# Reordering the early steps, the softmax steps and the first two output blocks of a hybrid attention block

## The chip, the cores and the metric

The kernel runs on one core of one Trainium2 chip. The metric is the device time of one execution in microseconds (us), the median over several runs. PE is TensorE, which multiplies matrices; DVE is VectorE, ACT is ScalarE, POOL is GpSimd, and SP issues transfers.

## What is computed

The reference is one decoder block over 512 positions of width 2048, in float32:

```
hn    = rmsnorm(x, norm1_g);  proj = hn @ w_in
o_a   = dilated_mixture(q_a, k_a, v_a)                # 8 heads, three dilated windows mixed by their sums
kc,vc = compress_blocks(k_c), compress_blocks(v_c)    # silu(flat @ w1) @ w2 over blocks of 32, stride 16
o_b   = sum of gates * (compressed, selected, window) # 8 heads, 2 groups of keys and values
h     = x + concat(rmsnorm(o_a), rmsnorm(o_b)) @ w_out
h     = h + (silu(hn2 @ w_gate) * (hn2 @ w_up)) @ w_down,  hn2 = rmsnorm(h)
out   = rmsnorm(h, final_g)
```

`compress_blocks` adds a position code to each of 32 positions of a block before the product with `w1`. All attention scores carry a distance penalty (`bias`).

## The kernel before

Everything is kept transposed: 128 features on the partitions, 512 positions on the free dimension. Each float32 operand is split into a high part (`h`, made by ACT as a rounded copy) and a low part (`l`, made by DVE as the difference), and a product is three matmuls: high times high, low times high, high times low (`mm3`, L165 to L167). `ah` and `al` hold the 16 blocks of the input of the current product, `wh` and `wl` the split weights.

The weights arrive in units of 512 KB (`raw`, four buffers, `load_to`). A unit is split in two halves of 128x512, each a `Job`: `first` is ACT's copy into `wh` (L136), `second` DVE's difference into `wl` (L139). `next_half` takes the next half for PE; before that it lets ACT split the half three further on and DVE the half two further on (`split_to`). `wh` and `wl` have five buffers each. `later(n, f)` puts `f` off to the start of the n-th half after the current one. The order of the units is written out by hand in `plan()`, and the scheduling is manual: each engine executes its instructions in the order in which the program emits them.

The stages touched:

1. After the input's norm factor `r1` is known (58.7 us into the profiled execution), the compression inputs are made from four PSUM banks `pc` in eight parts (`kv_part`): DVE multiplies a bank by `r1` (L333, `tmp`), adds position codes into `ku` (L341), ACT rounds it into `kvs` (L343), DVE takes the low part (L328). The parts are run from `side_hook`, one after every second column block of a projection. `gates_out` multiplies the gate projection `pg` by `r1` (L360) and transposes it on PE (L363, `pgt`). Meanwhile PE computes the projections ks, kw, vs and vw (`pp`), each in two units of 24 matmuls, and between them 16 units of the compression weights `w1` (`phid`, L382 and L383); `W1_AFTER` says how many follow each unit. `compressed` turns the result (`phidt`, two Silu, `pcmp`) when ten and twelve units are done. After each projection `evac` multiplies by `r1` and splits (L431, L437, L438).
2. Eight times, PE computes four projections and, between every six matmuls of them (`step`), one step of the attention heads in hand: scores of a tile (`s`, or `cmp_s` in the compressed branch), transposes of the exponentials (`t`), products with the values (`pv`, tile `po`). In a score step DVE adds the bias and takes the row minimum (L502, L551), ACT takes the exponential and its sum (L504, L554), and DVE inverts the sum and scales (L477 to L482, L556 to L559). A tile that was scored is transposed three steps later at the earliest (`SLACK`).
3. When the last head's value projection is half done, `split_act` turns the outputs `osb` of mixer B into the inputs `ah`, `al` 0 to 7 of the output projection (L254, L255), two per half. The output projection (`pab`) runs over 16 blocks for these inputs, two halves of four inputs each, while the last heads still take their steps, and later over 16 blocks for the other eight inputs. `close_attention` computes the group norms when all heads are done.
4. The feed-forward part follows, from 700 us to the end; nothing of it is changed.

Of the kernel before, what the change touches and what calls it, by code (L numbers as in the profile page):

```python
# [11 lines left out]
F32 = mybir.dt.float32  # L12
F32R = mybir.dt.float32r
AF = mybir.ActivationFunctionType
OP = mybir.AluOpType
# [3 lines left out]
KB = D // 128  # L19
# [16 lines left out]
NCMP = 31  # L36
MH, ML, WH, WL = 32, 32, 16, 16


W1_AFTER = {"ks": (0, 0), "kw": (3, 3), "vs": (3, 3), "vw": (2, 2)}  # L40


def plan():
# [28 lines left out]
def block_kernel(ctx: ExitStack, tc: tile.TileContext, xt, wst, wdn, smalls, wg, w2c, bias, ident_in, out):  # L72
# [76 lines left out]
                jobs.append(Job(half_of(u, k), load=lambda u=u: load_to(u + 1), even=True))  # L149

    n_plain = len(jobs)
    total = n_plain + 14 * FB + KB * NPH

    def split_to(n):
# [28 lines left out]
    def later(n, f):  # L183
        i = len(lag)
        while i and lag[i - 1][0] > pos["half"] + n:
            i -= 1
        lag.insert(i, (pos["half"] + n, f))
# [5 lines left out]
    def run_unit(subs):  # L193

        for k in range(0, len(subs), 4):
            h, l = next_half()
            for s in range(4):
                o, mh, ml, st, sp_ = subs[k + s]
                mm3(o, h[:, 128 * s:128 * s + 128], l[:, 128 * s:128 * s + 128], mh, ml, st, sp_)
                if s % 2:  # L200
                    side_hook[0]()
# [73 lines left out]
    def tmp(name="tmp"):  # L275
        return ap_.tile([128, S], F32, tag="tmp", name=name, bufs=3)
# [53 lines left out]
    def kv_part(s, g, v):  # L330
        if not v:
            kv_src[0] = tmp()
            dve.tensor_tensor(kv_src[0], pc[2 * s + g], r1, op=OP.mult)  # L333
        tv = kv_src[0].rearrange("p (c i) -> p i c", i=16)
        c = (SM_PK, SM_PV)[s] + 16 * v
        u = cp.tile([128, S], F32, tag="ku", name="ku", bufs=2)
        uv = u.rearrange("p (i c) -> p i c", i=16)
        n = 32 - v
        if v:
            pool_e.memset(uv[:, :, 31:], 0.0)  # L340
        dve.tensor_tensor(uv[:, :, :n], tv[:, :, v:], sm[:, c:c + 16, None].to_broadcast([128, 16, n]), op=OP.add)  # L341
        h, l = (kvs[:, s, v, :, i, g, :] for i in range(2))
        act.activation(h, uv, AF.Copy)  # L343
        kv_low()
        pend.append((l, uv, h))
# [9 lines left out]

    side_hook[0] = task

    def gates_out():
        t = tmp()
        dve.tensor_tensor(t[:48, :], pg[:48, :], r1[:48, :], op=OP.mult)  # L360
        p = ps.tile([128, 4, 128], F32, tag="misc", name="pgt")
        for b in range(4):
            pe.transpose(p[:, b, :48], t[:48, 128 * b:128 * b + 128], ident[:48, :48])  # L363
        act.activation(gates, p[:, :, :24], AF.Copy)
        dve.tensor_tensor(gates, gates, p[:, :, 24:48], op=OP.add)
        act.activation(gates, gates, AF.Sigmoid)
# [96 lines left out]
    class Att:  # L463
# [20 lines left out]
        def s(self, tiles):  # L484
            p = ps.tile([128, 512], F32, tag="sc", name="psc", bufs=2)
            e = late["pool"].tile([128, 128 * sum(t + 1 for t in tiles)], F32, tag=f"e{tiles[0]}", name="e")
            st = late["pool"].tile([128, 4], F32, tag="st", name="st", bufs=4)
            o = 0
            qh, ql = self.q[:2]
            kh, kl = self.k  # L490
            for t in tiles:
                n = 128 * max(t + 1, 2)
                mm3(p[:, o:o + n], qh[:, 128 * t:128 * t + 128], ql[:, 128 * t:128 * t + 128],
                    kh[:, :n], kl[:, :n], True, True)
                o += n
            o = 0
            oe = 0
            for c, t in enumerate(tiles):
                n = 128 * (t + 1)
                et = e[:, oe:oe + n]  # L500
                m, den = st[:, 2 * c:2 * c + 1], st[:, 2 * c + 1:2 * c + 2]
                dve.tensor_tensor_reduce(et, p[:, o:o + n], self.bias[:, 384 - 128 * t:512], 1.0, 3e38,  # L502
                                         OP.add, OP.min, m)
                act.activation(et, et, AF.Exp, bias=m, scale=-1.0, accum_out=den)  # L504
                self.scale_rows(et, den, t, self.kind == "win")
                self.e[t] = et
                o += 128 * max(t + 1, 2)
                oe += n

        def t(self, tiles):  # L510
            p = ps.tile([128, 512], F32, tag="t", name="pt", bufs=2)
# [30 lines left out]
        def cmp_s(self):  # L542
            p = ps.tile([128, 512], F32, tag="sc", name="psc", bufs=2)
            e = late["pool"].tile([128, 4, 32], F32, tag="ec", name="ec")
            e3 = late["e3"]
            st = late["pool"].tile([128, 16], F32, tag="stc", name="stc", bufs=2)
            q = self.q[2]
            for t in range(4):
                pe.matmul(p[:, 32 * t:32 * t + 32], q[:, 128 * t:128 * t + 128], self.k, start=True, stop=True)
            for t in range(4):  # L550
                dve.tensor_tensor_reduce(e[:, t, :NCMP], p[:, 32 * t:32 * t + NCMP],  # L551
                                         self.bias[:, 512 + 32 * t:512 + 32 * t + NCMP], 1.0, 1e29, OP.add,
                                         OP.min, st[:, t:t + 1])
                act.activation(e[:, t, :NCMP], e[:, t, :NCMP], AF.Exp, bias=st[:, t:t + 1], scale=-1.0,  # L554
                               accum_out=st[:, 4 + t:5 + t])
            dve.tensor_scalar(st[:, 4:8], st[:, 4:8], 1e-30, None, op0=OP.max)  # L556
            dve.reciprocal(st[:, 4:8], st[:, 4:8])
            for t in range(4):
                dve.tensor_scalar(e3[:, t, :, :NCMP], e[:, t, None, :NCMP].to_broadcast([128, 3, NCMP]),  # L559
                                  st[:, 4 + t:5 + t], gates[:, t, self.gate:self.gate + 1],  # L560
                                  op0=OP.mult, op1=OP.mult)

        def cmp_t(self):
            p = ps.tile([128, 512], F32, tag="t", name="pt", bufs=2)
# [10 lines left out]

    queue = deque()
    now = [0]
    cur = {"s": None, "t": None, "ready": deque(), "turn": 0}
    SLACK = 2

    def step():

        now[0] += 1
        for _ in range(2):
            turn = cur["turn"]
            cur["turn"] ^= 1
            if turn == 0:
                if cur["t"] is None and cur["ready"] and cur["ready"][0][0] + SLACK < now[0]:
                    cur["t"] = cur["ready"].popleft()[1]
                    cur["ti"] = 0  # L590
                    cur["tat"] = -9
                a = cur["t"]
                if a is not None:
                    is_pv = cur["ti"] == len(a.t_steps) - 1
                    if is_pv and (cur["tat"] + SLACK > now[0] or (a.v is not None and not a.v.ready())):
                        continue
                    a.t_steps[cur["ti"]]()
                    cur["tat"] = now[0]
                    cur["ti"] += 1
                    if cur["ti"] == len(a.t_steps):  # L600
                        cur["t"] = None
                    return True
            else:
                if cur["s"] is None and queue and len(cur["ready"]) == 0:
                    if isinstance(queue[0], Att):
                        cur["s"] = queue.popleft()
                        cur["si"] = 0
                    else:
                        queue.popleft()()
                        return True  # L610
                a = cur["s"]
                if a is not None:
                    t = cur["t"]
                    if t is not None and t.kind != "cmp" and a.kind != "cmp" and cur["ti"] <= cur["si"]:
                        continue
                    a.s_steps[cur["si"]]()
                    cur["si"] += 1
                    if cur["si"] == len(a.s_steps):
                        cur["s"] = None
                        cur["ready"].append((now[0], a))  # L620
                    return True
        return False
# [71 lines left out]
    for j in range(NH):  # L694
# [25 lines left out]
        for half in range(2):  # L720
            in_unit(p, half)
            if j == NH - 1 and half == 0:
                for i in range(8):
                    later(i // 2, lambda i=i: split_act(i, osb[:, 8 + i, :], sm[:, SM_GB + i:SM_GB + i + 1]))
        t = evac_v(p)
# [160 lines left out]
    side_hook[0] = last_steps  # L886
    term = {}
    pab = []
    for nb in range(KB):
        while "hs" not in rest and (nb == 4 and not idle() or nb == 2 and (queue or cur["s"])):  # L890
            step()
        p = out_unit(1, ("proj", "sc", "t")[nb // 2 % 3])
        if "hs" in rest:
            later(0, lambda nb=nb, p=p: add_b(nb, p))
        else:
            pab.append((nb, p))
# [355 lines left out]
```

## Time and profile before

| | |
|---|---|
| Median of 3 runs | 2183.11 us (2182.37 to 2186.63) |
| Profiled execution, its own time | 2182.41 us |
| Its span in the trace | 2180.6 us |
| Granted TensorE clock, mean | 0.998 |
| PE, DVE, ACT, POOL busy | 2161.7, 1568.4, 970.5, 43.7 us |
| Read from and written to HBM | 225.51 MB, 4.19 MB |

Times inside the execution count from the start of the span. A row of the order of time gives the start, the duration, the engine, the line, the operation, what it writes and reads, the shape and the count; in brackets stands how long the engine was idle before it and what ended that. A row of the waits gives who waited for whom: us in total, times, and the longest. A row of the table by stretches gives the stretch, its length, the busy time of PE, PE's weight loads, DVE, ACT and POOL with the number of instructions, the granted clock, the share of the DMA engines and GB/s.

### The profile page before, as it was taken

The numbers are of one execution on the slowest core, as the hardware profiler recorded it, in microseconds if no ns is written. First come the engines' busy times: TensorE is split into PE (matmuls) and PEld (weight loads), VectorE is DVE, ScalarE is ACT, GpSimd is POOL, SyncE is SP. The second block draws the span as 40 slices with busy tenths as digits, with TensorE's granted clock in tenths as the row PEclk, the third lists the DMA queues.
The fourth block names the chain that finished last, engine by engine and source line by source line (L and its number), as shares of the span: only waits on it lengthen the run. The fifth ranks groups of instructions, "written<-read, shape, count | busy, mean of one in ns | idle before, by whom it ended". The sixth has DMA issues, their size and how long they took to land.

```text
span 2180.6 us, 39719 instructions
## 1 busy us (share of the span) xinstructions
PE 2161.7 (99%) x15776; PEld 2021.7 (93%) x15776; DVE 1568.4 (72%) x3046; ACT 970.5 (45%) x1862; POOL 43.7 (2%) x51
## 2 busy tenths in 40 slices
PE   9999999999999999999999999999999999999997
PEld 7788888888887889999999999999999999999997
DVE  6755666356667578979687786869596877868686
ACT  6544444244444255535344443535353444435356
POOL 0000000000000000000000000000000000000003
PEclk9999999999999999999999999999999999999999
DMA  6442222322134334343333333333333333333233
GB/s 223 145 138 80 80 81 68 99 90 80 58 100 154 97 97 107 117 117 93 107 112 108 96 117 102 112 88 117 117 98 107 108 112 93 117 107 108 80 125 107
DMA packets 81866, 232.28 MB, mean 107 GB/s; under 512 B 8848, under 2 KB 11536, under 8 KB 81680
## 3 DMA queue, kind: packets, MB, share of 16 engines
q1 hardware_dynamic: 80960, 228.17, 33.2%
q0 software_dynamic: 720, 1.57, 0.5%
q8 instruction: 124, 2.03, 0.4%
q14 instruction: 62, 0.51, 0.1%
HBM read 225.51 MB, written 4.19 MB: 105 GB/s over the span
## 4 chain that ended last, share of the span: by engine, by line
PE 96%; DVE 2%; ACT 1%; issue 0%; DMA 0%; SPq 0%; DVEq 0%; ACTq 0%
PE P L1012 15%; PE P L1010 15%; PE P L1011 15%; PE pp L165 6%; PE pp L167 6%; PE pp L166 6%; PE pd L1011 4%; PE pd L1010 4%; PE pd L1012 4%; PE pab L166 3%; PE pab L167 3%; PE pab L165 3%; PE pt L515 1%; PE psc L167 1%; PE psc L166 1%; PE psc L165 1%
## 5 line engine op out<-in xcount | busy, mean ns | idle before, releaser
L136 ACT ACTIVATE wh<-raw 128x512 fp32r<-128x512 f32 x888 | 549.2, 628 | 533.5 <-PE P L1011 209.6
L139 DVE TENSOR_TENSOR wl<-raw,wh 128x512 fp32r<-128x512 f32 x888 | 596.5, 685 | 47.4 <-ACT wh L136 46.9
L1012 PE MATMUL P<-ah,wl 128*128 128x256 f32 x1552 | 428.9, 276 | 0.3 <-DVE wl L139 0.3
L1010 PE MATMUL P<-ah,wh 128*128 128x256 f32 x1552 | 428.8, 276 | 0.0
L1011 PE MATMUL P<-al,wh 128*128 128x256 f32 x1552 | 428.8, 276 | 0.0
L1012 PEld LDWEIGHTS P<-ah,wl 128*128 128x128 f32 x1552 | 291.4, 188 | 0.5 <-DVE wl L139 0.5
L1011 PEld LDWEIGHTS P<-al,wh 128*128 128x128 f32 x1552 | 291.4, 188 | 0.0
L1010 PEld LDWEIGHTS P<-ah,wh 128*128 128x128 f32 x1552 | 291.4, 188 | 0.0
L165 PE MATMUL pp<-ah,wh 128*128 128x512 f32 x640 | 260.5, 407 | 0.0
L167 PE MATMUL pp<-ah,wl 128*128 128x512 f32 x640 | 251.0, 392 | 0.0
L166 PE MATMUL pp<-al,wh 128*128 128x512 f32 x640 | 250.3, 391 | 0.0
L754 DVE TENSOR_TENSOR raw<-raw 128x512 f32<-128x512 f32 x346 | 237.3, 686 | 3.4
L1010 PE MATMUL pd<-ah,wh 128*128 128x256 f32 x784 | 216.6, 276 | 0.0
L1012 PE MATMUL pd<-ah,wl 128*128 128x256 f32 x784 | 216.6, 276 | 0.0
L1011 PE MATMUL pd<-al,wh 128*128 128x256 f32 x784 | 216.5, 276 | 0.0
L136 ACT ACTIVATE wh<-rawd 128x512 fp32r<-128x512 f32 x160 | 101.2, 632 | 247.8 <-PE pd L1011 123.5
L1078 DVE TENSOR_TENSOR hs<-hs,pd 128x512 f32<-128x512 f32 x98 | 67.4, 688 | 122.9 <-PE pd L1012 122.7
L1011 PEld LDWEIGHTS pd<-al,wh 128*128 128x128 f32 x784 | 147.2, 188 | 0.0
L1010 PEld LDWEIGHTS pd<-ah,wh 128*128 128x128 f32 x784 | 147.2, 188 | 0.0
L1012 PEld LDWEIGHTS pd<-ah,wl 128*128 128x128 f32 x784 | 147.2, 188 | 0.0
L167 PEld LDWEIGHTS pp<-ah,wl 128*128 128x128 f32 x640 | 120.2, 188 | 27.9
L139 DVE TENSOR_TENSOR wl<-rawd,wh 128x512 fp32r<-128x512 f32 x160 | 110.1, 688 | 40.7 <-ACT wh L136 35.6
(275 smaller groups left out, 4565.4 us busy)
## 6 DMA issues: line engine op xcount, KB each, us to landing
raw<-in_wst_dram SPq DMA_DIRECT2D x310, 512.0 KB, 3.5
rawd<-in_wdn_dram SPq DMA_DIRECT2D x160, 256.0 KB, 2.6
bias<-in_bias_dram SPq DMA_DIRECT2D x16, 320.0 KB, 3.0
xc<-in_xt_dram SPq DMA_DIRECT2D x16, 256.0 KB, 3.3
hs<-in_xt_dram SPq DMA_DIRECT2D x16, 256.0 KB, 5.0
fin<-in_wdn_dram SPq DMA_DIRECT2D x8, 512.0 KB, 3.9
out_dram<-hs SPq DMA_DIRECT2D x8, 256.0 KB, 2.1
out_dram<-scaled SPq DMA_DIRECT2D x3, 512.0 KB, 2.8
```

The source lines that it names most:

```text
L136: act.activation(self.h, self.src(), AF.Copy)
L139: dve.tensor_tensor(self.l, self.src(), self.h.bitcast(F32), op=OP.subtract)
L165: pe.matmul(o, wh, mh, start=start, stop=False)
L166: pe.matmul(o, wh, ml, start=False, stop=False)
L167: pe.matmul(o, wl, mh, start=False, stop=stop)
L515: pe.transpose(p[:, 128 * (o + b):128 * (o + b) + 128], self.e[t][:, 128 * b:128 * b + 128], ident)
L754: return lambda: dve.tensor_tensor(o(), o(), x(), op=OP.add)
L1010: pe.matmul(o, wh, mh, start=start, stop=False, skip_group_check=True)
L1011: pe.matmul(o, wh, ml, start=False, stop=False, skip_group_check=True)
L1012: pe.matmul(o, wl, mh, start=False, stop=stop, skip_group_check=True)
L1078: dve.tensor_tensor(hs[:, nb, :], hs[:, nb, :], p, op=OP.add)
```

## The change

Five things are reordered; the number of matmuls and transfers stays.

- The 16 compression units are distributed anew: 0, 3, 4, 3, 3, 3 after kw's first and second, vs's first and second and vw's first and second unit, where it was 3, 3, 3, 3, 2, 2.
- `tmp` of the compression inputs is written with its two inner dimensions exchanged, so that the reads for `ku` are contiguous and the write of `tmp` is not.
- The product of `pg` and `r1` becomes a task of its own, the third of the nine that `side_hook` runs, ahead of `gates_out`.
- In a score step all minima come first, then all exponentials; the inversion and scaling are put off by `later(0, ...)`, and so come behind the next weight split on DVE.
- The first two output blocks are computed in turn: inputs 0 to 3 for both, then inputs 4 to 7 for both. Their weight jobs are exchanged accordingly. For the last head `pv` is put off by one more step (`late`).

On the engines' queues this gives: SP's and POOL's order is the same. ACT's order changes at the compression inputs and, near the end of the attention, by one weight copy moved ahead. PE's order changes from kw to vw and over the first five output blocks. DVE's order changes at the compression inputs and in every score step.

```diff
-W1_AFTER = {"ks": (0, 0), "kw": (3, 3), "vs": (3, 3), "vw": (2, 2)}
+W1_AFTER = {"ks": (0, 0), "kw": (0, 3), "vs": (4, 3), "vw": (3, 3)}
...
     n_plain = len(jobs)
+    k = 2 * units.index(("out", 0, 1))
+    jobs[k + 1], jobs[k + 2] = jobs[k + 2], jobs[k + 1]
...
     def kv_part(s, g, v):
         if not v:
             kv_src[0] = tmp()
-            dve.tensor_tensor(kv_src[0], pc[2 * s + g], r1, op=OP.mult)
-        tv = kv_src[0].rearrange("p (c i) -> p i c", i=16)
+            dve.tensor_tensor(kv_src[0].rearrange("p (i c) -> p c i", i=16),
+                              pc[2 * s + g].rearrange("p (c i) -> p c i", i=16),
+                              r1.rearrange("p (c i) -> p c i", i=16), op=OP.mult)
+        tv = kv_src[0].rearrange("p (i c) -> p i c", i=16)
...
+    gated = []
+
+    def gates_in():
+        gated.append(tmp())
+        dve.tensor_tensor(gated[0][:48, :], pg[:48, :], r1[:48, :], op=OP.mult)
+
+    tasks.insert(2, gates_in)
+
     def gates_out():
-        t = tmp()
-        dve.tensor_tensor(t[:48, :], pg[:48, :], r1[:48, :], op=OP.mult)
+        t = gated[0]
...
+            todo = []
             for c, t in enumerate(tiles):
                 n = 128 * (t + 1)
-                et = e[:, oe:oe + n]
+                et = self.e[t] = e[:, oe:oe + n]
                 m, den = st[:, 2 * c:2 * c + 1], st[:, 2 * c + 1:2 * c + 2]
                 dve.tensor_tensor_reduce(et, p[:, o:o + n], self.bias[:, 384 - 128 * t:512], 1.0, 3e38,
                                          OP.add, OP.min, m)
-                act.activation(et, et, AF.Exp, bias=m, scale=-1.0, accum_out=den)
-                self.scale_rows(et, den, t, self.kind == "win")
-                self.e[t] = et
+                todo.append((et, m, den, t))
                 o += 128 * max(t + 1, 2)
                 oe += n
+            for et, m, den, t in todo:
+                act.activation(et, et, AF.Exp, bias=m, scale=-1.0, accum_out=den)
+
+            def rows():
+                for et, m, den, t in todo:
+                    self.scale_rows(et, den, t, self.kind == "win")
+
+            later(0, rows)
...
-    cur = {"s": None, "t": None, "ready": deque(), "turn": 0}
+    cur = {"s": None, "t": None, "ready": deque(), "turn": 0, "late": 0}
...
-                    if is_pv and (cur["tat"] + SLACK > now[0] or (a.v is not None and not a.v.ready())):
+                    if is_pv and (cur["tat"] + SLACK + cur["late"] > now[0] or (a.v is not None and not a.v.ready())):
...
             if j == NH - 1 and half == 0:
+                cur["late"] = 1
...
-    for nb in range(KB):
+    first = [ps.tile([128, 512], F32, tag="proj", name="pab", bufs=2) for _ in range(2)]
+    run_unit([(first[n], ah[:, 4 * k + s, :], al[:, 4 * k + s, :], k == 0 and s == 0, k == 1 and s == 3)
+              for k in range(2) for n in range(2) for s in range(4)])
+    pab.extend(enumerate(first))
+    for nb in range(2, KB):
```

The score step of the compressed branch (`cmp_s`) is changed in the same way: its four minima first, then the four exponentials, then the scalings in a `rows` of its own, put off by `later(0, rows)`.

More of the change, by code (lines that the diff above doesn't have):

```diff
@@ L553, in cmp_s, with rows @@
                                          OP.min, st[:, t:t + 1])
+            for t in range(4):
                 act.activation(e[:, t, :NCMP], e[:, t, :NCMP], AF.Exp, bias=st[:, t:t + 1], scale=-1.0,
                                accum_out=st[:, 4 + t:5 + t])
[L556 to L561, printed above, removed]
+            def rows():
+                dve.tensor_scalar(st[:, 4:8], st[:, 4:8], 1e-30, None, op0=OP.max)
+                dve.reciprocal(st[:, 4:8], st[:, 4:8])
+                for t in range(4):
+                    dve.tensor_scalar(e3[:, t, :, :NCMP], e[:, t, None, :NCMP].to_broadcast([128, 3, NCMP]),
+                                      st[:, 4 + t:5 + t], gates[:, t, self.gate:self.gate + 1],
+                                      op0=OP.mult, op1=OP.mult)
+            later(0, rows)
         def cmp_t(self):
```

## The prediction

> **What bounds the kernel now.** I read the page first (busy shares and the chain that ended last), then the table by stretches, then the waits of PE alone, and then the order of time around each of those waits.
>
> ```profile
> PE 2161.7 (99%) x15776; PEld 2021.7 (93%) x15776; DVE 1568.4 (72%) x3046; ACT 970.5 (45%) x1862; POOL 43.7 (2%) x51
> ...
> PE 96%; DVE 2%; ACT 1%; issue 0%; DMA 0%; SPq 0%; DVEq 0%; ACTq 0%
> ```
> ```profile
> 82.00:140.00 58.00, 57.22 (x321) 49.19 (x320) 32.76 (x57) 28.79 (x56) 0.00 (x0) 1.00 0.68 227
> 140.00:640.00 500.00, 500.00 (x2512) 419.94 (x2511) 290.48 (x800) 217.60 (x538) 15.86 (x12) 1.00 0.25 80
> ```
> ```profile
> PE pab L166 <- DVE al L255: 1.6, 2, 0.9
> PE phid L383 <- DVE wl L139: 1.6, 2, 1.1
> ```
> PE is the bound: 2161.7 of 2180.6 us, at a granted clock of 1.00 (the column behind POOL's). The change adds and removes no matmul, so it can only move the few microseconds in which PE stands still. The row 140 to 640 has PE busy for 500.00 of 500.00 us: in the attention heads, where most of the edited lines run, there is nothing to win. The two waits lie in stretches whose order changes: the first output blocks (pab) and the first compression run (phid). A third, of the gates' transposes (pgt), stands in the order of time below.
>
> A matmul is drawn longer than the spacing to the next, so idle time understates a stall. I measure start to start, less the undisturbed spacing.
>
> ```profile
> 64.74 0.39 PE L166 MATMUL pp<-al,wh 128*128 128x512 f32 x1
> 64.97 0.39 PE L167 MATMUL pp<-ah,wl 128*128 128x512 f32 x1
> 66.63 0.42 PE L363 MATMUL pgt<-ident,tmp 48*128 48x48 f32 x4 [1.27 <-ACT kvs L343]
> ...
> 77.99 0.28 PE L382 MATMUL phid<-wh,kvs 128*128 128x256 f32 x1
> 79.33 0.33 PE L383 MATMUL phid<-wl,kvs 128*64 128x256 f32 x1 [1.06 <-DVE wl L139]
> ...
> 79.62 0.28 PE L383 MATMUL phid<-wl,kvs 128*64 128x256 f32 x1
> 79.73 0.28 PE L382 MATMUL phid<-wh,kvs 128*128 128x256 f32 x1
> 80.53 0.33 PE L383 MATMUL phid<-wl,kvs 128*64 128x256 f32 x1 [0.52 <-DVE wl L139]
> ...
> 108.75 0.28 PE L382 MATMUL phid<-wh,kvs 128*128 128x256 f32 x1
> 109.11 0.34 PE L383 MATMUL phid<-wl,kvs 128*64 128x256 f32 x1
> ```
> Spacing is 0.23 us at 512 columns (64.74 to 64.97) and 0.11 for phid (79.62 to 79.73). Stalls: gates 1.66 - 0.23 = 1.43; first compression run (1.34 - 0.11) + (0.80 - 0.11) = 1.92; at 108.75, 0.36 - 0.11 = 0.25.
>
> ```profile
> 658.16 0.39 PE L167 MATMUL pab<-ah,wl 128*128 128x512 f32 x1
> 658.93 0.49 PE L165 MATMUL po<-et_h,vwh 128*128 128x512 f32 x1 [0.38 <-ACT et_h L523]
> ...
> 662.20 0.39 PE L167 MATMUL pab<-ah,wl 128*128 128x512 f32 x1
> 662.69 0.49 PE L165 MATMUL pab<-ah,wh 128*128 128x512 f32 x1
> 663.94 0.50 PE L166 MATMUL pab<-al,wh 128*128 128x512 f32 x1 [0.75 <-DVE al L255]
> ...
> 665.56 0.47 PE L165 MATMUL pab<-ah,wh 128*128 128x512 f32 x1
> 666.89 0.50 PE L166 MATMUL pab<-al,wh 128*128 128x512 f32 x1 [0.86 <-DVE al L255]
> ```
> Less 0.23 each: po 0.54; then 0.26, 1.02 and 1.10 for the fifth and seventh of the attention inputs (ah, al). Together 2.92. All told 1.43 + 1.92 + 0.25 + 2.92 = 6.52 us.
>
> **Gates' factor.** The transposes wait for DVE's product of pg and r1, queued as tenth since r1 came, behind four compression parts. It becomes the fifth, so it is done some 3 us before PE gets there. After it DVE's next link is the sum of the gates, 0.73 us behind the transposes as before. I take all 1.43.
>
> **Compression inputs, and the run that now starts later.**
>
> ```profile
> 58.72 0.69 DVE L333 TENSOR_TENSOR tmp<-pc,r 128x512 f32<-128x512 f32 x1 [4.28 <-ACT r L246]
> ...
> 59.75 0.39 PE L165 MATMUL pp<-ah,wh 128*128 128x512 f32 x1
> ...
> 61.33 0.70 DVE L328 TENSOR_TENSOR kvs<-ku,kvs 128x512 fp32r<-128x512 f32 x1
> 61.93 0.70 DVE L333 TENSOR_TENSOR tmp<-pc,r 128x512 f32<-128x512 f32 x1
> 62.66 1.03 DVE L341 TENSOR_TENSOR ku<-tmp,sm 128x512 f32<-128x512 f32 x1
> ...
> 67.36 0.25 DVE L365 TENSOR_TENSOR gates<-gates,pgt 128x96 f32<-128x96 f32 x1 [0.84 <-ACT gates L364]
> 67.53 0.68 DVE L139 TENSOR_TENSOR wl<-raw,wh 128x512 fp32r<-128x512 f32 x1
> ...
> 76.59 0.69 DVE L431 TENSOR_TENSOR tmp<-pp,r 128x512 f32<-128x512 f32 x1
> 77.98 0.69 DVE L438 TENSOR_TENSOR ksl<-tmp,ksh 128x512 fp32r<-128x512 f32 x1 [0.70 <-ACT ksh L437]
> 78.59 0.69 DVE L139 TENSOR_TENSOR wl<-raw,wh 128x512 fp32r<-128x512 f32 x1
> ```
> L333 wrote tmp straight and the eight ku sums read it 64 bytes apart, at 1.03 us. Now four L333 write 128 bytes apart and the ku sums read straight. No row shows a strided write. Bounds: 0.69 (straight, L333) and 1.03 (strided read, L341); I take 1.03, the only strided row, for the four writes, and 0.69 for the sums. [...]
>
> The first matmul of ks (59.75) takes the bank that the first L333 empties, now at 59.41; 0.34 later is 59.75, and with 0.05 for the release PE loses some 0.06.
>
> The first run of compression weights moves behind kw's second half, 24 matmuls later, and DVE has 5.5 us more for it. What is late next is kw's second half itself, whose low part is the third DVE weight split after the gates. With the gates' stall gone, the sum of the gates is at 67.36 - 1.43 = 65.93 and the first split 0.17 later, at 66.10. From there the new order has ten operations at 0.60 (61.33 to 61.93) and two strided L333, each 1.03 and 0.04 before the sum that reads it: 6.00 + 2.14, so L431 is at 74.24. From it to ksl is 1.39, to the split 0.61, its length 0.69, and PE follows 0.05 behind: 76.98. PE wants it at 77.99 - 1.43 + 2 x 0.23 = 77.02. It just fits. Bounds: with L333 at 0.69 there is 0.7 to spare; if L341 is slow for its broadcast operand and stays at 1.03, four more of 0.34 make a stall of 1.3. I take 0.1.
>
> So the 1.92 goes, and 0.1 + 0.06 comes. The 0.25 at 108.75 stands behind a table load and two Silu that sat inside a run; they move to a run's end, in front of 5.5 us of matmuls. It goes.
>
> The runs are now 3, 4, 3, 3, 3 units. A run needs a DVE split (0.60) per 0.45 us of PE (four matmuls of 0.11), and four halves can stand ready in the five buffers; over the eight halves of the longest run DVE falls back 8 x 0.15 = 1.2 us against 4 x 0.60 in hand. No stall.
>
> **First two output blocks.** Both now take inputs 0 to 3 first (24 matmuls), then 4 to 7.
>
> ```profile
> 655.68 0.16 DVE L478 RECIPROCAL st<-st 128x1 f32<-128x1 f32 x1 [0.78 <-ACT e L504]
> 655.88 0.42 DVE L480 TENSOR_SCALAR e<-e,st 128x384 f32<-128x384 f32 x1
> ...
> 656.82 1.42 DVE L255 SCALAR_TENSOR_TENSOR al<-osb,sm,ah 128x512 fp32r<-128x512 f32 x2
> 658.15 0.42 DVE L524 TENSOR_TENSOR et_l<-pt,et_h 128x256 fp32r<-128x256 f32 x1
> 658.91 0.29 DVE L524 TENSOR_TENSOR et_l<-pt,et_h 128x128 fp32r<-128x128 f32 x1 [0.34 <-ACT et_h L523]
> ...
> 665.38 2.12 DVE L255 SCALAR_TENSOR_TENSOR al<-osb,sm,ah 128x512 fp32r<-128x512 f32 x2 [0.23 <-ACT ah L254]
> ```
> The product po moves six matmuls on (the longer slack), to 658.16 + 7 x 0.23 = 659.77. What it needs gets later too: in the new order L478 and L480 (0.54) stand behind the two al instead of using DVE's wait for ACT, so the last et_l ends at 658.91 + 0.29 + 0.54 = 659.74, and the second matmul of po reads it at 660.0. It fits by 0.26; I keep 0.1 for it. Then po (2.1, 658.93 to some 661.05), 12 matmuls of block 1 (2.7) and two groups of transposes (0.7) stand ahead of the fifth input: PE reaches it at 665.3, where its low part was released at 663.94 even on the old times; and the seventh at 667.0 with its low part at 667.2, released at 666.89. DVE loses 0.54 but no longer waits twice for ACT in the last pair of exponentials (0.7 and 0.6), so these times hold or improve. All 2.92 goes.
>
> The closing steps follow six to twelve matmuls later. The seventh block needs block 0's bank back, three DVE operations (2 us) after the second broadcast; 36 matmuls (8 us) lie between them instead of 48. No cost.
>
> **Scalings behind the next split.** In the heads the change puts one wl split ahead of the reciprocal and the scaling. DVE stood idle there waiting for the exponentials:
>
> ```profile
> 328.20 0.17 DVE L556 TENSOR_SCALAR stc<-stc 128x4 f32<-128x4 f32 x1 [1.07 <-ACT ec L554]
> ```
> The split (0.60) fits into 1.07, so the compressed branch's scalings, whose readers on PE start with nothing to spare, keep their time. The other scalings are read three steps (18 matmuls, 4 us) later or more. Net 0, bounds +0.5 and -0.5.
>
> **Sum.** Profiled execution: 2182.4 us (span 2180.6 and 1.8 around it), 0.7 under the median of the runs, 2183.1. 2182.4 - 6.52 + 0.06 + 0.1 + 0.1 = 2176.1 us. About 0.2% (4.4 us) is what a measurement of this kernel can tell from no change.
>
> **Rivals.**
> (a) DVE is late for kw's second half: broadcast, not stride, makes L341 slow, or a strided write costs twice the strided read's excess. Stall 1.3, up to 2.5 with both: 2177.4 to 2178.6. For it: the margin of 0.04. Against: L328 has a three-level pattern too and takes 0.70. Chance 0.15.
> (b) The scalings come late: DVE takes its queue in order, so a split whose wh is not ready holds the scaling behind it. At 0.60 for each of eight heads, 4.8: 2180.9. It decides once the split's wait exceeds the 0.47 left of the 1.07. Against: that split's wh is made a half before the exponentials. Chance 0.06. [...]
> (c) Slower: the compression runs become bound by their transfers, as 16 units are drawn together behind kw. Past the four units loaded ahead, 16 x 0.5 MB must come within 16 x 0.9 + 4 x 5.5 = 37 us, 227 GB/s, which is just what the row 82 to 140 moved on average. At 150 GB/s it would be 56 us: 2176.1 + 19 = 2195. It decides below some 175 GB/s (48 us), where the 6.3 won are lost and 4.4 more. Against: PE had no wait for a transfer there. Chance 0.07.
> (d) The output blocks do not gain: some al still comes as late as PE does, half of 2.92 stays, and a part of (a): 2178 to 2179.5. Chance 0.07.
>
> **How the numbers follow.** Forecast 0.65 (2175 to 2177.5). Ends: 2174.6, if the small costs are nothing (0.26), the heads give 0.5 and the runs scatter by the 0.7 above, to 2181.0, which takes in (a), (b) and (d); (c) and a little more stay out. Faster by over 0.2% is below 2178.0: the forecast and most of (a), 0.77. Within 0.2%: the rest of (a), (b), (d), 0.15. Slower: (c) and what I do not see, 0.08.
>
> **What would show it.** Right: no PE wait at pgt; none of phid or pab on DVE; kw's second half without a gap; L341 at 0.69 and L333 near 1.03; DVE's idle time before L478 down, PE in the heads unchanged. Wrong: a gap of over 0.5 us at kw's second half, waits of pt for ecs or e, wh waiting for raw with PE idle after it, or a PE wait at al that has only moved.

## The result, and the profile after

The changed kernel takes 2175.82 us (median of 6 runs, 2175.39 to 2176.22), the kernel before 2183.18 in the same session (6 runs, 2182.37 to 2187.25): a ratio of 0.9962, 95% interval 0.9949 to 0.9974. The profiled execution took 2175.4 us against 2182.4. The forecast was 2176.1, and the change is faster by more than 0.2%, as forecast.

The page after, and the table by stretches for the kernel after, then two rows of the same table for before that were not shown yet:

```profile
PE 2159.9 (99%) x15776; PEld 2021.9 (93%) x15776; DVE 1566.0 (72%) x3046; ACT 965.9 (44%) x1862; POOL 42.7 (2%) x51
...
PE 98%; DVE 1%; ACT 0%; DMA 0%; issue 0%; SPq 0%; DVEq 0%; ACTq 0%
```
```profile
58.00:82.00 24.00, 24.00 (x106) 18.70 (x105) 21.23 (x32) 11.12 (x20) 0.38 (x3) 1.00 0.13 40
82.00:140.00 58.00, 57.11 (x332) 49.75 (x331) 34.67 (x66) 32.74 (x66) 0.00 (x0) 1.00 0.68 222
140.00:640.00 500.00, 500.00 (x2513) 420.14 (x2513) 289.21 (x797) 213.62 (x539) 15.43 (x12) 1.00 0.25 82
640.00:690.00 50.00, 50.00 (x262) 42.43 (x261) 36.38 (x85) 27.88 (x55) 2.64 (x2) 1.00 0.29 90
```
```profile
58.00:82.00 24.00, 21.15 (x100) 16.33 (x98) 21.50 (x31) 12.74 (x22) 0.38 (x3) 1.00 0.10 27
640.00:690.00 50.00, 47.91 (x247) 39.42 (x246) 34.75 (x86) 28.59 (x58) 3.22 (x2) 1.00 0.23 75
```

The work is the same (15776 matmuls in both; PE busy 2161.7 and 2159.9 us). PE's idle time in 58 to 82 and in 640 to 690 is gone: 24.00 of 24.00 and 50.00 of 50.00, where it was 21.15 and 47.91. The heads, 140 to 640, are as they were. 82 to 140 gained nothing (57.11 where it was 57.22).

The waits of PE after, those that are left in the changed stretches:

```profile
PE pcmp L423 <- DVE et_h L427: 0.7, 1, 0.7
...
PE phid L394 <- DVE wl L139: 0.2, 1, 0.2
```

No wait of pgt, po or pab is left, and one short one of phid. Idle time understates a stall (a 512-column matmul is drawn at 0.39 us and the next starts 0.23 behind it), so I summed over the trace how much later each matmul starts after its neighbour than is usual (the median for a neighbour of that tile and shape). These sums are called the excess below. From before to after the excess fell from 5.85 to 2.24 us in the first 140 us, and from 3.70 to 0.33 in 640 to 700. Elsewhere it moved by at most 0.4 (140 to 640: 2.18 to 2.00; 700 to 880: 1.81 to 2.18; later: 7.46 to 7.40). Together that is -6.9 of the 7.0 us. Some of it lies ahead of every edit: in the first 60 us the excess fell from 0.78 to 0.37, and the first changed instruction starts at 58.08 instead of 58.72. Over the fourteen traces of this case that start lies anywhere from 57.85 to 58.94, so these 0.64 us are scatter and not a gain of the change.

The order of time after, where the gates and kw's second half stand:

```profile
58.08 1.10 DVE L335 TENSOR_TENSOR tmp<-pc,r 128x512 f32<-128x512 f32 x1 [4.28 <-ACT r L248]
...
61.23 0.68 DVE L366 TENSOR_TENSOR tmp<-pg,r 48x512 f32<-48x512 f32 x1
...
64.57 0.39 PE L169 MATMUL pp<-ah,wl 128*128 128x512 f32 x1
...
64.89 0.44 PE L374 MATMUL pgt<-ident,tmp 48*128 48x48 f32 x4
...
74.11 0.68 DVE L442 TENSOR_TENSOR tmp<-pp,r 128x512 f32<-128x512 f32 x1
...
76.10 0.68 DVE L139 TENSOR_TENSOR wl<-raw,wh 128x512 fp32r<-128x512 f32 x1
...
76.51 0.39 PE L168 MATMUL pp<-al,wh 128*128 128x512 f32 x1
...
76.84 0.50 PE L169 MATMUL pp<-ah,wl 128*128 128x512 f32 x1
```

The gates' product is done at 61.91, three microseconds before the transposes read it, and pgt follows 0.32 us behind the last matmul. The low part of kw's second half ends at 76.78, and the matmul that reads it starts 0.33 us behind the one before it, 0.10 more than the usual 0.23. It just fits, as forecast.

The output blocks after:

```profile
655.82 0.39 PE L167 MATMUL po<-et_h,vwh 128*128 128x512 f32 x1
...
656.21 0.69 DVE L454 TENSOR_TENSOR tmp<-pp,r 128x512 f32<-128x512 f32 x1
...
657.73 0.40 PE L167 MATMUL pab<-ah,wh 128*128 128x512 f32 x1
...
658.28 1.42 DVE L257 SCALAR_TENSOR_TENSOR al<-osb,sm,ah 128x512 fp32r<-128x512 f32 x2 [0.78 <-ACT ah L256]
...
661.29 0.48 PE L167 MATMUL pab<-ah,wh 128*128 128x512 f32 x1
```

The matmul at 661.29 is the first of the fifth input, whose low part (the first of the two al from 658.28) has been there for two microseconds. L454 at 656.21 is a row that the prediction did not look at; the experiments show why it matters.

In some executions of six of the kernels here the feed-forward part starts slowly (256-column matmuls 0.118 us apart instead of 0.113 until some 985 us, 511 instead of 532 in the 60 us from 920), which adds some 4 us wherever the edit is, so where a kernel's times fall in two groups both are given.

### The profile page after: what moved, and what is told of

It reads as the page before. It is cut to its first block, busy times and chain, and to the rows that moved or that the text cites. A ratio compares the mean times of both kernels' runs of the same rounds, so it can differ in the third digit from the quotient of the medians.

```text
span 2173.6 us, 39728 instructions
## 1 busy us (share of the span) xinstructions
PE 2159.9 (99%) x15776; PEld 2021.9 (93%) x15776; DVE 1566.0 (72%) x3046; ACT 965.9 (44%) x1862; POOL 42.7 (2%) x51
## 4 chain that ended last, share of the span: by engine, by line
PE 98%; DVE 1%; ACT 0%; DMA 0%; issue 0%; SPq 0%; DVEq 0%; ACTq 0%
PE P L1040 15%; PE P L1038 15%; PE P L1039 15%; PE pp L167 7%; PE pp L169 7%; PE pp L168 7%; PE pd L1040 4%; PE pd L1039 4%; PE pd L1038 4%; PE pab L169 3%; PE pab L167 3%; PE pab L168 3%; PE pt L533 1%; PE po L168 1%; PE psc L169 1%; PE po L167 1%
```

## The experiments

Parts alone, on the kernel before, and parts undone, on the kernel after. Times of before in these sessions have medians of 2182.8 to 2182.9 us. An interval of a ratio is about 2 us wide to each side, so the traces carry the reading.

**The gates' factor alone.**

```
+        dve.tensor_tensor(gated[0][:48, :], pg[:48, :], r1[:48, :], op=OP.mult)
...
+    tasks.insert(2, gates_in)
```

> The kernel before with the gates' product as third task, nothing else. My theory: PE's 1.43 us stall before the gates' transposes goes, and DVE's later chain shifts with PE, so the 1.92 us in the first compression run stays: 1.4 us less than before. Rival (the DVE queue is what is short there, the stall only moves into the compression run): no gain, the phid waits grow from 1.6 to about 3.

Measured: 2183.94 us (2183.14 to 2184.32), ratio 1.0003 (0.9993 to 1.0012). No gain. The order of time of this kernel:

```profile
77.35 0.33 PE L390 MATMUL phid<-wl,kvs 128*64 128x256 f32 x1 [0.78 <-DVE wl L139]
...
77.75 0.27 PE L389 MATMUL phid<-wh,kvs 128*128 128x256 f32 x1
80.31 0.34 PE L390 MATMUL phid<-wl,kvs 128*64 128x256 f32 x1 [2.29 <-DVE wl L139]
```

The gates' stall is gone, and PE arrives that much earlier at the first compression run, whose weights DVE splits no sooner: two stalls of 0.95 and 2.44 us, 3.39 in place of 1.92. The rival was right. On top came something neither theory had, in the table by stretches of this kernel (the column behind POOL's is the granted clock):

```profile
78.66:82.07 3.41, 1.76 (x12) 1.45 (x12) 3.25 (x7) 3.40 (x7) 0.00 (x0) 1.00 0.23 59
82.07:85.48 3.41, 3.41 (x14) 2.98 (x13) 2.76 (x5) 1.15 (x2) 0.00 (x0) 0.50 0.89 274
```

For 3.41 us behind the stalls TensorE was granted half its clock (0.50 in the second row), and phid's matmuls started 0.21 us apart (82.39, 82.61, 82.82) instead of 0.11. The stalls by themselves (3.39 against 1.43 + 1.92) would have left the time as it was; the median stands 1.1 us higher.

**The runs alone.**

```
-W1_AFTER = {"ks": (0, 0), "kw": (3, 3), "vs": (3, 3), "vw": (2, 2)}
+W1_AFTER = {"ks": (0, 0), "kw": (0, 3), "vs": (4, 3), "vw": (3, 3)}
```

> The kernel before with the compression units distributed 0, 3, 4, 3, 3, 3, nothing else. My theory: the 1.92 us of the first compression run go, but without the earlier gates' product and the straight reads DVE's weight split for kw's second half ends at 79.28 where PE wants it at 78.45, so 0.88 us of stall appear there: 1.0 us less than before. Rival (24 matmuls more are enough for DVE): 1.9 us less, and no wait at kw's second half.

Measured: 2181.25 us (2180.57 to 2181.94), ratio 0.9991 (0.9982 to 1.0). The two stalls of the first run are gone, the gates' 1.43 stays, kw's second half waits for 0.88 us, and 0.34 appears at 104.36 where 0.25 was at 108.75. The theory holds: the stall is the 0.88 that it named. The median fell by 1.6 where 1.0 was expected, less than such medians can tell apart.

**The order of the compression inputs alone.**

```
-            dve.tensor_tensor(kv_src[0], pc[2 * s + g], r1, op=OP.mult)
+            dve.tensor_tensor(kv_src[0].rearrange("p (i c) -> p c i", i=16),
+                              pc[2 * s + g].rearrange("p (c i) -> p c i", i=16),
+                              r1.rearrange("p (c i) -> p c i", i=16), op=OP.mult)
```

> The kernel before with tmp written strided and read straight, nothing else. My theory: a strided write costs 1.10 us, a straight sum 0.69; per compression input that is 0.4 more and 2 x 0.36 less, so DVE is 0.3 us per input earlier: the gates' stall shrinks from 1.43 to about 1.0 and the compression run's by about 0.6 more: 1.0 us less than before. Rival (write and read cost the same, nothing is won): 0.

Measured: 2181.78 us (2181.19 to 2182.64), ratio 0.9993 (0.9984 to 1.0003). The stalls shrink from 1.43 and 1.92 to 0.86 and 1.38 (0.70 + 0.68), 1.1 us in all, and the median is 1.1 lower. This is as expected (1.0).

**Gates and layout together**, to see whether the shorter DVE work saves the gates' gain, and whether the clock drops again.

```
+    tasks.insert(2, gates_in)
...
+            dve.tensor_tensor(kv_src[0].rearrange("p (i c) -> p c i", i=16),
+                              pc[2 * s + g].rearrange("p (c i) -> p c i", i=16),
...
```

> The kernel before with two parts, the gates' factor and the order of the compression inputs; runs, softmax steps and output blocks as before. The gates alone left two stalls of TensorE in the first compression run, 0.95 and 2.44 us, and the granted clock fell right after; the layout alone took 1.1 us out of the stalls there. Theory (the granted clock falls only because the stalls come so close together that TensorE is idle for over half of some 3.4 us): the two stalls come to about 3.4 - 1.1 = 2.3 us, the clock stays whole, and the time is that of the layout alone less nothing, 2181 to 2182 us. Rival (the drop needs less than that): the stalls are 2.3 us but the clock is granted at half again, and the time is 2183 us. Second rival (the units' order is not what the gates need): no stall of over 0.5 us is left, 2180 us.

Measured: 2182.90 us (2182.17 to 2183.71), ratio 0.9999 (0.9989 to 1.0009). The stalls came to 0.44 + 2.11 = 2.55 us and the clock was halved all the same, from this kernel's table:

```profile
75.98:79.39 3.41, 1.19 (x8) 0.66 (x7) 3.26 (x7) 2.13 (x5) 0.00 (x0) 1.00 0.02 5
79.39:82.80 3.41, 3.41 (x17) 3.41 (x18) 3.41 (x6) 1.79 (x4) 0.00 (x0) 0.51 0.73 205
```

My theory, that these stalls would not do it, is refuted; the first rival gave the time to 0.1 us. The half of some 3.4 us in it was my estimate, which no run had shown. PE was busy for 1.19 of the 3.41 us ahead of the drop, in the gates alone for 1.76. The last section sets these stretches beside one without a drop.

**Layout undone.** The change without the exchanged dimensions.

```
-            dve.tensor_tensor(kv_src[0].rearrange("p (i c) -> p c i", i=16),
...
+            dve.tensor_tensor(kv_src[0], pc[2 * s + g], r1, op=OP.mult)
```

> The changed kernel with tmp written straight and read strided as before. My theory: DVE's chain up to the split for kw's second half takes 4 x 0.36 - 2 x 0.41 = 0.6 us longer and the margin there was 0.1 to 0.2, so PE waits some 0.45 us at pp on wl, less 0.1 at the first matmul of ks: 0.3 us more than the changed kernel. Rival (there was more room than I worked out): no change.

Measured: 2176.66 us (2176.16 to 2177.1, and one of 2181.06, the profiled one), ratio 0.9971 (0.9961 to 0.9981). kw's second half now waits for 0.62 us (0.45 expected) and the time is 0.8 us above the whole change (0.3 expected). This kernel holds gates and runs, so those two do work together: what the gates need is the later run, not the shorter DVE work.

**Runs of eight.** The whole change with all compression units in two runs, and the turning steps moved with them.

```
-W1_AFTER = {"ks": (0, 0), "kw": (0, 3), "vs": (4, 3), "vw": (3, 3)}
+W1_AFTER = {"ks": (0, 0), "kw": (0, 8), "vs": (0, 8), "vw": (0, 0)}
-                        if n1 in (10, 12):
+                        if n1 in (8, 9):
```

> The changed kernel with the 16 compression units in two runs of eight, behind kw's and vs's second unit; the turning of the first result starts behind the first run. Theory of the splits: DVE falls back 0.15 us per half, 2.4 us over 16 halves, against four halves (2.4 us) in hand, so a run of eight just fits and the time stays within 0.6 us. Rival, transfers: four units are loaded ahead, the seventh and eighth can only be asked for when a buffer comes free inside the run and land 3.5 to 4.5 us later, so PE stands still for 2 to 3 us per run of eight, with wh waiting for raw: 4 to 6 us more than the changed kernel.

Measured: 2186.92 us (2183.68 to 2193.23), ratio 1.0027 (1.0017 to 1.0036): slower than before, and 11.1 us above the whole change, where the rival had 4 to 6. The waits of PE, then rows of the order of time, then the table, all of this kernel:

```profile
PE phidt L403 <- ACT osb L397: 2.3, 1, 2.3
PE phid L394 <- DVE wl L139: 1.9, 6, 0.3
```
```profile
90.55 1.16 ACT L136 ACTIVATE wh<-raw 128x512 fp32r<-128x512 f32 x2 [0.47 <-DMA raw<-in_wst_dram]
...
94.42 0.63 ACT L136 ACTIVATE wh<-raw 128x512 fp32r<-128x512 f32 x1 [0.65 <-DMA raw<-in_wst_dram]
94.96 0.37 ACT L397 ACTIVATE osb<-phid 128x256 f32<-128x256 f32 x1
95.34 1.28 ACT L409 ACT_TABLE_LOAD   x1
95.38 0.90 PE L403 MATMUL phidt<-ident,osb 128*128 128x64 f32 x3 [2.25 <-ACT osb L397]
```
```profile
86.00:94.40 8.40, 5.93 (x35) 3.96 (x33) 6.29 (x10) 5.33 (x10) 0.00 (x0) 1.00 0.90 313
94.40:101.30 6.90, 5.92 (x18) 5.05 (x19) 3.28 (x6) 4.08 (x8) 0.00 (x0) 0.51 0.48 163
```

In a run of eight both supplies give out. ACT waits for the transfer (0.47 and 0.65 us, at 313 GB/s), phid for DVE's split, and ACT's copy L397, which PE's transposes need, stands in its queue behind a weight copy that itself waited for the transfer. The clock is at half for 6.8 us (0.51 over the 6.90 us of the second row). So the short supply that the prediction's slower rival feared exists in runs of eight, mixed with the other two causes; how the 11.1 us divide among them was not taken apart. The runs of three and four stay clear of it.

**The two output blocks alone** (with the later value product).

```
+    jobs[k + 1], jobs[k + 2] = jobs[k + 2], jobs[k + 1]
+    run_unit([(first[n], ah[:, 4 * k + s, :], al[:, 4 * k + s, :], k == 0 and s == 0, k == 1 and s == 3)
+              for k in range(2) for n in range(2) for s in range(4)])
```

> The kernel before with the first two output blocks in turn and the last products put off by one step, nothing else. My theory: the four stalls at po and at the fifth and seventh input go whatever DVE's order is: 2.9 us less than before. Rival (they need the scalings behind the weight splits as well): at most 1.5 less, with a PE wait left at al.

Measured: 2184.20 us (2183.88 to 2185.99, and one of 2179.56), ratio 1.0003 (0.9994 to 1.0012). The tenth is 3.3 under before's median of 2182.9; of the nine above, the profiled one has the slow start of the feed-forward part in its trace. The times alone therefore show no gain, and the trace has to tell. There the excess of 640 to 700 falls from 3.70 to 1.46, by 2.24 and not by all of it as the theory had it; the rival is not right either, as no wait at al is left. The order of time of this kernel shows what is left:

```profile
661.51 0.29 DVE L482 TENSOR_SCALAR e<-e,st 128x128 f32<-128x128 f32 x1
661.71 1.32 ACT L256 ACTIVATE ah<-osb,sm 128x512 fp32r<-128x512 f32 x2
661.72 0.68 DVE L445 TENSOR_TENSOR tmp<-pp,r 128x512 f32<-128x512 f32 x1
...
662.45 0.50 PE L167 MATMUL pab<-ah,wh 128*128 128x512 f32 x1 [0.86 <-DVE tmp L445]
```

Block 1 is now begun 12 matmuls earlier than in the kernel before, and its accumulator is the PSUM bank that still holds the last value projection `pp`. DVE empties it with L445, and L445 stands behind the scaling L482, ahead of which DVE waits 0.56 us for ACT's exponential. A stall of 1.02 us.

**The softmax steps alone.**

```
-                self.scale_rows(et, den, t, self.kind == "win")
+            later(0, rows)         # rows: scale_rows for each tile, behind the next weight split
```

> The kernel before with all minima, then all exponentials, the scalings behind the next weight split, nothing else. My theory: the eight heads give nothing (PE busy 500.0 of 500 us from 140 to 640); at the first output blocks po's wait grows by 0.5 and the al waits shrink by 1.0 to 1.6, as DVE no longer waits twice for ACT: 0.8 us less than before (0.3 to 1.3). Rival 1 (the scalings come late for the transposes): several us more, PE waits at pt. Rival 2: exactly no change.

Measured: 2183.18 us (2181.87 to 2186.91), ratio 1.0003 (0.9993 to 1.0012). Seven of the ten times (2181.87 to 2183.42) stand where before stands. The excess of 640 to 700 is 3.47, only 0.23 less; 0.8 was expected. Heads unchanged.

**Softmax steps undone**, and **the output blocks undone**, each from the whole change.

```
-            later(0, rows)
+                self.scale_rows(et, den, t, self.kind == "win")
```

> The changed kernel with the softmax steps in the order of before. My theory: with the output blocks in turn the fifth and seventh input have over 1 us in hand, so nothing changes: within 0.3 us of the changed kernel. Rival (the softmax order carries part of the gain): 0.8 to 1.5 us more.

Measured: 2177.16 us (2176.59 to 2177.90), ratio 0.9971 (0.996 to 0.9982), 1.3 above the whole change. "No change" is refuted; the same stall is back in its trace, [0.86 <-DVE tmp L454] at 659.05, where L454 runs at 658.31 behind the scaling instead of 656.21.

```
-    jobs[k + 1], jobs[k + 2] = jobs[k + 2], jobs[k + 1]
-    for nb in range(2, KB):
+    for nb in range(KB):
```

> The changed kernel with the output blocks one after the other as before. My theory: the stalls come back, less what the softmax order takes off them: 2.1 us more than the changed kernel (1.6 to 2.9), with PE waits at po and al. Rival (the softmax order alone removes them): no change.

Measured: 2179.40 us (2178.16 to 2179.65, and two of 2182.9 and 2183.5), ratio 0.9982 (0.9973 to 0.9992). 3.6 us above the whole change, more than the 2.1 expected: with the scalings put off and no blocks in turn, the excess of 640 to 700 is 3.46, so that order helps nothing there.

**Softmax steps and output blocks together**, the first 140 us as before.

```
+            later(0, rows)
+    for nb in range(2, KB):        # blocks 0 and 1 in turn ahead of it
```

> The kernel before with two parts, the softmax steps in rows and the two output blocks in turn with the later value product; gates, compression inputs and runs as before. Theory (these two need each other and nothing else): the output part loses all of its 3.4 us of stalls though either alone took out 2.2 and 0.2, the first 140 us stay as before, and the time is about 3.4 us less than before, 2179.0 to 2179.5 us (the executions in which the feed-forward part starts slowly stand up to 4 us above). Rival (the block in turn is held by the weights, whose supply the earlier parts set): some 1 us of stall is left, 2180.2 us.

Measured: 2179.60 us (2178.92 to 2180.27, and two of 2183.4 and 2183.8, one of them the profiled one), ratio 0.9985 (0.9975 to 0.9994). The excess of 640 to 700 is 0.32. Blocks alone took off 2.24, softmax alone 0.23, both 3.4. The theory holds. With the runs above, the two halves of the change add up: early part alone (the output blocks undone, which still holds the softmax steps) 2179.4, late part alone 2179.6, both 2175.8, neither 2182.9.

**A version built on the findings.** The whole change with runs of 3, 4, 3, 3, 3 turned into 4, 4, 3, 3, 2, the turning steps one unit later, and the second value product in a PSUM bank of its own.

```
-W1_AFTER = {"ks": (0, 0), "kw": (0, 3), "vs": (4, 3), "vw": (3, 3)}
+W1_AFTER = {"ks": (0, 0), "kw": (0, 4), "vs": (4, 3), "vw": (3, 2)}
-                        if n1 in (10, 12):
+                        if n1 in (11, 13):
+                if g:
+                    p2 = ps.tile([128, 512], F32, tag="o", name="pcmp")
```

> The changed kernel with two stalls taken out that it still has: the units 0, 4, 4, 3, 3, 2, so that the copy of the first result on ACT stands at the end of a run and not ahead of the weight copies in it (0.34 us), the turning steps after 11 and 13 units, and the second value product in a PSUM bank of its own (0.84 us). My theory: 1.1 us less than the changed kernel. Rival (a first run of four is too early for DVE): the phid wait moves to the first run, 0.3 to 0.8 less.

Measured: 2175.52 us (2174.77 to 2175.70, 5 runs), ratio 0.9966 (0.9953 to 0.9978). The stalls of pcmp (0.84) and of phid at 102 (0.34) are gone from the trace; 0.19 and 0.16 are new at 86.3 and 87.0, and this execution lost 0.87 us at its very start (8.8 to 9.5 us), ahead of any edit. Between 60 and 140 us the excess is 1.34 against 1.87. So 1.1 us less was expected, 0.5 shows in the stretch that was edited, and the 0.3 us in the medians can't be told from none.

## Why the prediction was right, step by step

**What bounds the kernel.** PE alone, and the stalls in four places: held. In the profiled pair 7.0 us came and 6.26 were forecast (6.52 less 0.26 of small costs). Of the difference, 0.64 is the earlier start ahead of every edit, which is luck. The rest is two misses that nearly cancel: small gaps beside the named ones went too (0.10 to 0.11 each around po and al, 0.45 in all), and 0.34 us of stall came where the sum had none. So the closeness of the total, 2175.82 against 2176.1, is in part luck; the stalls below are what bears the prediction out.

**Gates' factor, 1.43.** All gone, but the reason given does not suffice. The prediction wrote it as a term of its own; alone it is worth nothing (2183.94), because DVE's weight splits, not the gates, end last some 11 us on. It pays only with the later run, as the layout undone shows, which holds both. The sum was right since it was made for the whole change.

**Compression inputs.** The terms of the sum were the strided write (1.03, bounds 0.69 and 1.03) and the straight read (0.69). The groups by line and shape, 57 to 80 us, of after and then of before (time in all and mean ns behind the bar):

```profile
L335 DVE TENSOR_TENSOR tmp<-pc,r 128x512 f32<-128x512 f32 x4 | 4.4, 1103 | 4.3 <-ACT r L248 4.3
L345 DVE TENSOR_TENSOR ku<-tmp,sm 128x512 f32<-128x512 f32 x4 | 2.8, 692 | 0.1
```
```profile
L341 DVE TENSOR_TENSOR ku<-tmp,sm 128x512 f32<-128x512 f32 x4 | 4.1, 1037 | 0.1
L333 DVE TENSOR_TENSOR tmp<-pc,r 128x512 f32<-128x512 f32 x4 | 2.8, 691 | 4.3 <-ACT r L246 4.3
```

The write took 1.10, outside the bounds by 0.07; the reads are 0.69, so the 64-byte stride, not the broadcast operand, was L341's price. The strided write (1.10 at 128 bytes) cost a little more than the strided read (1.04 at 64 bytes); both took 0.69 straight. The first matmul of ks lost 0.13 instead of 0.06.

**The later run.** kw's second half was to be released at 76.98 and wanted at 77.02, cost 0.1. Its matmul started at 76.84 and lost 0.10. The chain of DVE operations was right almost link for link (L442 at 74.11, forecast 74.24).

**The 0.25 at 108.75** was to go. That stall went, but 0.34 came at 102.00, which the sum put at nothing; this step failed. Order of time, before and then after:

```profile
106.10 1.28 ACT L398 ACT_TABLE_LOAD   x1
...
107.70 2.71 ACT L136 ACTIVATE wh<-raw 128x512 fp32r<-128x512 f32 x5
```

```profile
100.78 0.39 ACT L397 ACTIVATE osb<-phid 128x256 f32<-128x256 f32 x1 [0.55 <-PE phid L394]
...
101.06 2.18 ACT L136 ACTIVATE wh<-raw 128x512 fp32r<-128x512 f32 x4
...
101.71 1.90 DVE L139 TENSOR_TENSOR wl<-raw,wh 128x512 fp32r<-128x512 f32 x3 [0.76 <-PE phid L394]
...
102.00 0.28 PE L393 MATMUL phid<-wh,kvs 128*128 128x256 f32 x1
...
102.46 0.34 PE L394 MATMUL phid<-wl,kvs 128*64 128x256 f32 x1 [0.18 <-DVE wl L139]
```

In the kernel before the blame was right: the weight copies stand behind the table load (106.10) and the Silu, and DVE's splits behind the copies. After, neither stands in front. ACT's copy of the first result (L397), due after eight units, now falls behind the first unit of a run; it waits for PE, and the weight copies behind it in ACT's queue come late. The prediction asked where the table load and the Silu would move, and not where this copy would. The kernel with the runs alone has the same 0.34. The version built on this, where the eighth unit ends a run, has no such stall.

**Output blocks, 2.92.** All gone, and 0.4 more. But the step's reason failed in one place. It said that the inputs would be early "even on the old times" of DVE, and so made the gain independent of the softmax order. The inputs were early; the wait that then came last was another, block 1's PSUM bank, which the step never listed. Blocks alone leave 1.02 us there. In the whole change L454 runs 2.1 us sooner because the scalings no longer stand in front of it. The prediction's remark that DVE "no longer waits twice for ACT" named the right cause for the wrong reader.

**Scalings in the heads, 0.** Right. The groups by line and shape, after and then before: DVE's idle time ahead of the reciprocal fell from 47.4 to 6.8 us over 96 of them, and PE did not gain from it.

```profile
L489 DVE RECIPROCAL st<-st 128x1 f32<-128x1 f32 x96 | 15.5, 161 | 6.8 <-ACT e L520 5.7
```
```profile
L478 DVE RECIPROCAL st<-st 128x1 f32<-128x1 f32 x96 | 15.7, 164 | 47.4 <-ACT e L504 46.3
```

Rival (b), scalings late, did not come: five waits of pt for ecs of 0.12 to 0.14 us stand in both traces alike. That DVE takes its queue in order the trace of before shows: behind its idle 1.07 us (to 328.20) stood a weight split whose `wh` was done at 325.21, and it ran at 329.61. In the same step after, the split stands ahead of the scaling, at 323.13, and 0.46 us of idle time are left. Rival (a) came to its margin and no further. Rival (c), the compression weights drawn together faster than they can be supplied, did not come in runs of three and four; runs of eight show it in part, at 11 us instead of 19, with DVE's splits and a halved clock in the price, and while 313 GB/s came in. The limit of 175 was worked out for the average of 37 us, and says nothing of so short a stretch.

## What to carry to other kernels

Where a kernel is bound by one engine at 99%, look for its few stalls one by one, and for each ask what ends second to last: an edit that removes one stall may only bring the engine sooner to the next, so such edits are to be costed and tried together. When accumulation is begun earlier, list who empties that PSUM bank, beside who makes the operands. An instruction that waits for another engine belongs behind the independent work of its queue, which may pay far away from the wait it shortens.

## What the runs showed of the hardware

**The granted clock.** In three kernels the granted clock fell to half in the middle of the execution: in the gates alone (0.50 from 82.07 to 85.48) and in gates and layout (0.51 from 79.39 to 82.80) for 3.41 us, behind two stalls less than half a microsecond apart, the longer of 2.44 and 2.11 us, and in the runs of eight (0.51 from 94.40 to 101.30) for 6.8 us, from within a wait of 2.3 us that follows several short ones. In gates and layout the 15 spacings of phid from 79.63 to 82.83 are 0.21 us instead of 0.11; by the spacing that is some 1.5 us lost behind a stall that was already paid for.

PE was busy, as drawn, for 1.76, 1.19 and 1.78 us of the 3.41 us ahead of the three drops. The stretch ahead of the drop in the runs of eight, and then a stretch of the kernel before, with its two stalls of the first compression run:

```profile
91.01:94.42 3.41, 1.78 (x12) 1.19 (x11) 2.43 (x4) 1.84 (x4) 0.00 (x0) 1.00 0.94 334
```
```profile
77.90:81.30 3.40, 1.82 (x12) 1.17 (x11) 3.32 (x6) 2.93 (x7) 0.00 (x0) 1.00 0.02 5
```

Behind the second no drop came: the clock is 1.00 in the next 3.41 us too, with PE busy throughout. Busy time as drawn is more than the matmuls' spacing adds up to: phid's are drawn at 0.28 us and start 0.11 us apart. So in the gates alone and in gates and layout the clock fell behind two close stalls of 3.39 and 2.55 us in all, and in the kernel before it did not behind two of 1.92; where the limit lies these runs do not show.

**The start of the feed-forward part.** Two rows of the table by stretches, output blocks alone and then the whole change, same work, same granted clock:

```profile
920.00:980.00 60.00, 60.00 (x511) 60.00 (x511) 45.07 (x75) 19.41 (x32) 0.00 (x0) 1.00 0.36 106
```
```profile
920.00:980.00 60.00, 60.00 (x532) 60.00 (x531) 45.83 (x75) 18.45 (x30) 0.00 (x0) 1.00 0.36 106
```

511 against 532 matmuls in 60 us with PE never idle. It ends near 985 us in the four traces that have it (the output blocks alone, the softmax steps alone, both together, layout undone), and costs some 4 us. Why was not found.
